# Layer 0's experts: per weight matrix all products of the latent tokens and all of the context tokens, one kind after the other

## The chip, the cores and the metric

One core of a Trainium2 chip runs the whole program. Its engines work side by side, each through its own list of instructions in order: TensorE (PE, matrix products; PEld is its weight loader), VectorE (DVE), ScalarE (ACT), GpSimd (POOL) and SyncE (SP), which issues most of the DMA transfers. The metric is the device time of one execution in microseconds (us), as the median of several.

## The reference

A network of two mixer layers, each followed by a layer of experts, and a second block behind them, all in float32. What matters here is the first layer of experts. It runs over two sets of tokens, 512 latent ones and 256 context ones, with the same 16 experts; each expert takes its best 64 latent tokens (`x`) and its best 32 context tokens (`ctx`).

```python
def expert_choice_ffn(h, router, w_gate, w_up, w_down):
    ...
    cap = CAPACITY_FACTOR * t // N_EXPERTS
    aff = jax.nn.softmax(h.astype(jnp.float32) @ router.astype(jnp.float32), axis=-1)
    gate, idx = lax.top_k(jnp.swapaxes(aff, 1, 2), cap)
    ...
    xs = h[bidx, idx]
    hid = jax.nn.silu(jnp.einsum('becd,edf->becf', xs, w_gate)) * jnp.einsum('becd,edf->becf', xs, w_up)
    y = jnp.einsum('becf,efd->becd', hid, w_down) * gate[..., None].astype(h.dtype)
    return jnp.zeros_like(h).at[bidx, idx].add(y)
```

Each expert has three matrices of 1024x1024: gate, up and down, 4 MB each.

## The kernel before

`moe0` is the stage of layer 0's experts. The tokens of an expert are the stationary operand, the weights stream past them. A matrix comes in four chunks of 1 MB (two row blocks of 128 rows each, `k0` = 0, 2, 4, 6). For each row block there are two latent products, each with 64 tokens against 512 columns of the weights, and four context products, each with 32 tokens against 256 columns. The two latent products write to partitions 0 and 64 on, so they stand side by side in the array; the four context products stand at 0, 32, 64 and 96. In the trace each product leaves two records, so a chunk shows as x8 latent records and x16 context records; in the listings of the program's order one row counts products, x4 and x8.

`expert_gemm` (line 852) runs over the chunks of one matrix: per chunk first the latent products (line 865), then the context ones (line 870), and then `st.done()`, which issues the load of a later chunk into the slot that comes next in a ring of slots. Loads go out on SP's queue (line 832) in the order in which the matrices are used; a load waits until the last product that read its slot is through.

Order of the matrices: gate and up of expert 0; then, for each further expert e+1, gate of e+1 (`product(0, e+1)`), down of e, up of e+1 (`product(1, e+1)`); last, down of expert 15. Results of gate go to `pl0`/`pc0`, of up to `pl1`/`pc1` (names in the trace: `pl`, `pc`), of down to `dl`/`dc` (tiles `ro_lg`). Around them:

- `glu` (line 1068): ACT applies silu to the gate results (into `hl`, `hc`), DVE multiplies by the up results.
- `hidden` (line 1077): TensorE transposes `hl` (four transposes) and `hc` (two), DVE and ACT copy them to `hT`, the stationary operand of the down matrix. It is called ahead of the last chunk of the next expert's gate matrix (`late`, `k == KD - 2`).
- `turn` (line 996): TensorE transposes the gathered tokens `xg` of expert e+2 (eight transposes), DVE and ACT write them to `xT`. It is called ahead of the last chunk of the up matrix.
- behind the down matrix DVE scales the results into `yl` and `yc`, and GpSimd adds them to the tokens in memory by an indirect transfer (lines 1129 to 1135). The stage after this one (retention) loads those tokens.

The order that is written in the code isn't quite the one that runs: a scheduler puts each engine's instructions in order when the program is built, by its own estimate of when their inputs are there, and may interleave what the code writes in sequence.

Of the kernel before, what the change touches and what calls it, by code (L numbers as in the profile page):

```python
# [6 lines left out]
F32 = mybir.dt.float32  # L7
# [4 lines left out]
AF = mybir.ActivationFunctionType  # L12
ALU = mybir.AluOpType
# [4 lines left out]
KD = 8  # L18
# [29 lines left out]
class Net:  # L48
# [658 lines left out]
    CL, CC, E = 64, 32, 16  # L707
# [144 lines left out]
    def expert_gemm(self, st, lat, con, outl, outc, swap=0, late=None, ws=None, done=True):  # L852

        nc = self.nc
        for k0 in range(0, KD, 2):
            w = st.get() if ws is None else ws[k0 // 2]
            if late is not None:
                late(k0)  # L860
            if lat is not None:
                for kk in (k0, k0 + 1):
                    for b in range(2):
                        c = b ^ swap
                        nc.tensor.matmul(outl[64 * b:64 * b + 64, :], lat(kk), w[:, kk - k0, 512 * c:512 * c + 512],  # L865
                                         start=kk == 0, stop=kk == KD - 1)
            if con is not None:
                for kk in (k0, k0 + 1):
                    for b in range(4):
                        nc.tensor.matmul(outc[32 * b:32 * b + 32, :], con(kk), w[:, kk - k0, 256 * b:256 * b + 256],  # L870
                                         start=kk == 0, stop=kk == KD - 1)
            if done:
                st.done()

    def moe0(self, yp, y):


        nc, I = self.nc, self.I
        i, CL, CC, E = 0, self.CL, self.CC, self.E
        CAP = CL + CC  # L880
        rp = self.pool("mo_r", side="right")
        m5l = rp.tile([128, 512], F32, name="mo_m5l")
        m5c = rp.tile([128, 256], F32, name="mo_m5c")
        ii = rp.tile([CAP, E], I32, name="mo_ii")
        si = rp.tile([128, 2, E], I32, name="mo_si")
        gc = rp.tile([128, 2, E], F32, name="mo_gc")
# [8 lines left out]
        g = [self.row(fp, self.modd[i][r, 2 * D:3 * D], f"po_g{r}") for r in range(2)]  # L895
# [32 lines left out]
        st = self.expert_stream(i, order + [(E - 1, "down")])  # L928
# [59 lines left out]
        wk = self.pool("mo_w", 2)  # L988
# [3 lines left out]
        xl2 = self.xl.rearrange("t (b n) -> (t b) n", b=2)  # L992
        xc4 = self.xc.rearrange("t (b n) -> (t b) n", b=4)
        A, B = self.ffnA[i], self.cols[i][:, 3]

        def turn(xg, xT, a=CL, b=CAP):

            for h in range(2):
                tp = tile4()
                for k in range(4):  # L1000
                    kk = 4 * h + k
                    nc.tensor.transpose(tp[:, k, 0:b], xg[:, 128 * kk:128 * kk + 128], self.ident[0:b, 0:b])
                for k in range(4):
# [12 lines left out]

        xT = Xp.tile([128, D], F32, name="X")[:, 0:KD * CL].rearrange("p (k t) -> p k t", k=KD)
        turn(xgs[0], xT, CL, CL)
        no = first(1)
        xg = gather(no, wk.tile([CAP, D], F32, name="xg")[0:CC])  # L1020
# [37 lines left out]
                nc.vector.tensor_copy(si[:, n, 1:E], tr[n][:, 1, 1:E])  # L1058
                nc.vector.tensor_copy(gc[:, n, 1:E], tr[n][:, 2, 1:E])

        def product(n, e, late=None):
            pl = ps.tile([128, 512], F32, name=f"pl{n}")
            pc = ps.tile([128, 512], F32, name=f"pc{n}")[:, 0:256]
            xT = xTs[e]
            self.expert_gemm(st, lambda k: xT[:, k, lat], lambda k: xT[:, k, con], pl, pc, late=late)
            glu(n, e, pl, pc)

        def glu(n, e, pl, pc):
            if n == 0:
                hid[e] = (wk.tile([128, 512], F32, name="hl"), wk.tile([128, 256], F32, name="hc"))  # L1070
                for h, p in zip(hid[e], (pl, pc)):
                    nc.scalar.activation(h, p, AF.Silu)
            else:
                for h, p in zip(hid[e], (pl, pc)):
                    nc.vector.tensor_tensor(h, h, p, ALU.mult)
# [12 lines left out]

        hid, xTs = {}, {}
        tokens = lambda e: gather(ii[:, e:e + 1], wk.tile([CAP, D], F32, name="xg"))  # L1090
        new = lambda: wk.tile([128, KD, CAP], F32, name="xT")
        ps = self.pool("mo_ps", 1, space=PSUM)
        xTc = wk.tile([128, KD, CAP], F32, name="xT")

        def second():
            indices()
            xgs.append(tokens(1))
        for n in range(2):
            ws = [st.get() for _ in range(4)]
# [9 lines left out]
            glu(n, 0, pl, pc)  # L1109
# [5 lines left out]
        xTs[1] = turn(xgs[1], new())  # L1115
        for e in range(E):
            if e + 2 < E:
                xg = tokens(e + 2)
            if e + 1 < E:
                product(0, e + 1, late=lambda k: hidden(e) if k == KD - 2 else None)  # L1120
            else:
                hidden(e)
            dl = psr.tile([128, 512], F32, name="ro_lg", bufs=2)
            dc = psr.tile([128, 512], F32, name="ro_lg", bufs=2)[:, 0:256]
            hTl, hTc = hid[e]
            self.expert_gemm(st, lambda k: hTl[:, k % 4, 64 * (k // 4):64 * (k // 4) + 64],
                             lambda k: hTc[:, k % 2, 32 * (k // 2):32 * (k // 2) + 32], dl, dc)
            yl = wk.tile([128, 512], F32, name="yl")
            nc.vector.scalar_tensor_tensor(yl, dl, gc[:, 0, e:e + 1], m5l, ALU.mult, ALU.mult)  # L1129
            nc.gpsimd.indirect_dma_start(out=xl2, out_offset=bass.IndirectOffsetOnAxis(ap=si[:, 0, e:e + 1], axis=0),  # L1130
                                         in_=yl, in_offset=None, compute_op=ALU.add)
            yc = wk.tile([128, 256], F32, name="yc")
            nc.vector.scalar_tensor_tensor(yc, dc, gc[:, 1, e:e + 1], m5c, ALU.mult, ALU.mult)
            nc.gpsimd.indirect_dma_start(out=xc4, out_offset=bass.IndirectOffsetOnAxis(ap=si[:, 1, e:e + 1], axis=0),
                                         in_=yc, in_offset=None, compute_op=ALU.add)
            if e + 1 < E:
                product(1, e + 1, late=lambda k: xTs.update({e + 2: turn(xg, new())}) if k == KD - 2 and e + 2 < E else None)
        self.warm(ps.tile([128, 512], F32, name="pl0"), yl, 7)
        ps.close()
        psr.close()  # L1140
# [4 lines left out]
        whb.close()  # L1145
        whp.close()
        rp.close()

    def moe1(self, yp, y):

# [1099 lines left out]
```

## Time and profile before

| | |
|---|---|
| median of 3 runs | 2636.24 us (2631.58 to 2636.72) |
| the profiled execution's own time | 2638.1 us |
| its span in the profile | 2636.3 us |
| TensorE busy | 2516.1 us, 95% of the span |
| stage of layer 0's experts 1 to 15 on TensorE | 571.11 to 1128.83 us of the span |

The rows that follow are from the one profiled execution. Times are microseconds from the start of the span. The busy time of TensorE counts a matrix product from its start to its modelled end, so products that overlap are not counted twice, and a small pause between products of two forms can be hidden in a busy engine.

### The profile page before, as it was taken

Reading aid. Unit: us, or ns where it says so; the run is one execution under the profiler, and the core shown is the slowest. Engines: PE = TensorE matmul, PEld = TensorE weight load, DVE = VectorE, ACT = ScalarE, POOL = GpSimd, SP = SyncE. Lnnn points to the kernel's source line nnn. Section 1 sums busy time; section 2 is a strip of 40 time slices with the busy share of each in tenths; the row PEclk is TensorE's granted clock in tenths of the full one; section 3 lists DMA queues with packets and bytes.
Section 4 is the critical chain, followed back from the end, with each engine's and each line's share of the span. In section 5 each row is a group of like instructions: output and inputs, shape, how many; then the busy total and the mean of one; then the engine's idle time right before and its main releaser. Section 6 shows DMA issues by size and latency. Waiting matters only on the chain. (4 is left out here: it accounts for less than half of the span.)

```text
span 2636.3 us, 36600 instructions
## 1 busy us (share of the span) xinstructions
PE 2516.1 (95%) x15122; PEld 1593.6 (60%) x15126; DVE 1089.3 (41%) x2121; ACT 690.5 (26%) x1335; POOL 557.1 (21%) x339
## 2 busy tenths in 40 slices
PE   7999998989999999999999999999998999999999
PEld 6777687833333333368877755444445766788887
DVE  5588686341111111152666332222235458433310
ACT  4322364421010110043224310100004336322211
POOL 2223224311111010023556200000001222122233
PEclk9999998989999999999999899999998999999999
DMA  7226604388999999442463589999982221133331
GB/s 252 80 65 214 234 2 169 137 322 325 395 399 399 390 386 374 156 134 70 146 238 128 218 334 420 419 419 420 419 365 81 98 100 33 56 96 96 120 104 56
DMA packets 145274, 584.80 MB, mean 222 GB/s; under 512 B 17671, under 2 KB 47535, under 8 KB 93908
## 3 DMA queue, kind: packets, MB, share of 16 engines
q1 hardware_dynamic: 138684, 569.87, 56.8%
q0 software_dynamic: 6416, 12.59, 2.2%
q8 instruction: 119, 1.95, 0.3%
q14 instruction: 47, 0.39, 0.0%
q10 hardware_dynamic: 8, 0.01, 0.0%
HBM read 567.70 MB, written 14.71 MB: 221 GB/s over the span
## 5 line engine op out<-in xcount | busy, mean ns | idle before, releaser
L276 POOL TENSOR_TENSOR wlo<-w,whi 128x1024 fp32r<-128x1024 f32 x103 | 271.0, 2632 | 610.6 <-ACT whi L275 610.4
L865 PE MATMUL pl<-w,xT 128*64 128x512 f32 x1240 | 293.0, 601 | 2.7 <-ACT hl L1308 2.7
L275 ACT ACTIVATE whi<-w 128x1024 fp32r<-128x1024 f32 x148 | 154.4, 1050 | 454.6 <-PE acc L296 189.4
L294 PE MATMUL acc<-whi,hhi 128*128 128x512 f32 (+2 forms) x672 | 265.7, 396 | 1.3 <-ACT pre L445 1.1
L295 PE MATMUL acc<-wlo,hhi 128*128 128x512 f32 (+2 forms) x672 | 261.0, 388 | 1.4 <-POOL wlo L276 1.4
L296 PE MATMUL acc<-whi,hlo 128*128 128x512 f32 (+2 forms) x672 | 260.0, 387 | 0.0
L296 PE MATMUL acc<-hhi,wlo 128*128 128x512 f32 (+2 forms) x528 | 198.7, 377 | 3.2 <-POOL wlo L276 3.2
L294 PE MATMUL acc<-hhi,whi 128*128 128x512 f32 (+2 forms) x528 | 198.8, 377 | 2.9 <-DVE hlo L289 1.5
L295 PE MATMUL acc<-hlo,whi 128*128 128x512 f32 (+2 forms) x528 | 199.1, 378 | 0.6 <-POOL hlo L406 0.5
L865 PEld LDWEIGHTS pl<-w,xT 128*64 128x64 f32 x1240 | 86.2, 137 | 149.1 <-issue 133.1
L276 DVE TENSOR_TENSOR wlo<-w,whi 128x1024 fp32r<-128x1024 f32 (+2 forms) x45 | 59.3, 1317 | 255.7 <-ACT whi L275 255.6
L865 PE MATMUL pl<-wb,xT 128*64 128x512 f32 x640 | 152.8, 599 | 0.0
L294 PEld LDWEIGHTS acc<-whi,hhi 128*128 128x128 f32 x672 | 127.5, 190 | 30.1 <-issue 6.1
L295 PEld LDWEIGHTS acc<-wlo,hhi 128*128 128x128 f32 x672 | 127.7, 190 | 27.0 <-POOL wlo L276 3.0
L296 PEld LDWEIGHTS acc<-whi,hlo 128*128 128x128 f32 x672 | 127.4, 190 | 25.5 <-issue 2.4
L164 DVE SCALAR_TENSOR_TENSOR ada_v<-w,csil,ada_v 128x1024 f32<-128x1024 f32 x84 | 132.8, 1616 | 7.6 <-DMA w<-in_ada_w_dram 6.2
L1766 POOL TENSOR_TENSOR X<-X,s_gf 128x1024 f32<-128x1024 f32 x2 | 4.7, 2364 | 515.5 <-DVE X L1292 506.8
L296 PEld LDWEIGHTS acc<-hhi,wlo 128*128 128x128 f32 (+1 forms) x528 | 98.2, 187 | 22.7 <-POOL wlo L276 3.4
L294 PEld LDWEIGHTS acc<-hhi,whi 128*128 128x128 f32 (+1 forms) x528 | 98.3, 186 | 22.4 <-DVE hlo L289 1.7
L295 PEld LDWEIGHTS acc<-hlo,whi 128*128 128x128 f32 (+1 forms) x528 | 98.5, 187 | 19.8 <-POOL hlo L406 0.7
L1012 ACT ACTIVATE xT<-ro_tp,cols,ffnA 128x32 f32<-128x32 f32 x128 | 43.7, 376 | 225.3 <-DVE xT L1009 222.6
L1130 POOL DMA_INDIRECT xl<-yl,mo_si x16 | 25.1, 1568 | 362.7 <-DVE yl L1129 360.9
(599 smaller groups left out, 4272.8 us busy)
## 6 DMA issues: line engine op xcount, KB each, us to landing
w<-in_moe_w_gate_dram SPq DMA_DIRECT2D x91, 1024.0 KB, 13.2
w<-in_moe_w_down_dram SPq DMA_DIRECT2D x84, 1024.0 KB, 14.0
w<-in_moe_w_up_dram SPq DMA_DIRECT2D x68, 1024.0 KB, 12.8
wb<-in_moe_w_up_dram SPq DMA_DIRECT2D x53, 1024.0 KB, 13.3
w<-in_ada_w_dram SPq DMA_DIRECT2D x40, 1024.0 KB, 6.2
wb<-in_moe_w_down_dram SPq DMA_DIRECT2D x38, 1024.0 KB, 11.3
wb<-in_moe_w_gate_dram SPq DMA_DIRECT2D x30, 1024.0 KB, 17.0
w<-in_ret_w_in_dram SPq DMA_DIRECT2D x16, 1024.0 KB, 5.5
```

The lines of the kernel that those rows point to most:

```text
L164: nc.vector.scalar_tensor_tensor(acc[r], w[:, kk], x, acc[r], ALU.mult, ALU.add)
L275: nc.scalar.activation(hi, raw[:, k:k + n, :], AF.Copy)
L276: (nc.vector if fast and (k // n) % 2 == 0 else nc.gpsimd).tensor_sub(lo, raw[:, k:k + n, :], hi.bitcast(F32))
L294: nc.tensor.matmul(out, lh[0], rh[0], start=start, stop=False)
L295: nc.tensor.matmul(out, lh[0], rh[1], start=False, stop=False)
L296: nc.tensor.matmul(out, lh[1], rh[0], start=False, stop=stop)
L865: nc.tensor.matmul(outl[64 * b:64 * b + 64, :], lat(kk), w[:, kk - k0, 512 * c:512 * c + 512], start=kk == 0, stop=kk == KD - 1)
L1012: nc.scalar.activation(xT[:, kk, a:b], tp[:, k, a:b], AF.Identity, scale=A[:, kk, 1:2], bias=B[:, kk, 1:2])
L1130: nc.gpsimd.indirect_dma_start(out=xl2, out_offset=bass.IndirectOffsetOnAxis(ap=si[:, 0, e:e + 1], axis=0), in_=yl, in_offset=None, comput ...
L1766: (nc.gpsimd if t % 3 else nc.vector).tensor_mul(x, x, gf)
```

## The change

In place of `expert_gemm` the three matrices of each expert go through a new function, `expert_runs`: one whole run over the four chunks with products of one kind, then a second run over the same four chunks with the other kind. Which kind comes first alternates from matrix to matrix, so that a matrix begins with the kind with which the one ahead of it ended. All four chunks of a matrix are held through the first run; `st.done()` is called in the second. `hidden` and `turn` are called between the two runs (`between`), and the steps behind the products (`glu`, the scaling and scatter) are called per kind, as soon as its run is through (`after`). Expert 0's own gate and up matrices still go through `expert_gemm`, which there had one kind per call already. (A further function that the change adds, `expert_hidden`, is not called anywhere.)

```diff
+    def latent_gemm(self, lat, w, k0, out, swap=0):
+
+        for kk in (k0, k0 + 1):
+            for b in range(2):
+                c = b ^ swap
+                self.nc.tensor.matmul(out[64 * b:64 * b + 64, :], lat(kk), w[:, kk - k0, 512 * c:512 * c + 512],
+                                      start=kk == 0, stop=kk == KD - 1)
+
+    def context_gemm(self, con, w, k0, out):
...
+    def expert_runs(self, st, lat, con, outl, outc, after, between=None):
...
+        kinds = (0, 1) if self.runs % 2 == 0 else (1, 0)
+        self.runs += 1
+        ws = []
+        for n, kind in enumerate(kinds):
+            if n and between is not None:
+                between()
+            for k0 in range(0, KD, 2):
+                if n == 0:
+                    ws.append(st.get())
+                w = ws[k0 // 2]
+                if kind == 0:
+                    self.latent_gemm(lat, w, k0, outl)
+                else:
+                    self.context_gemm(con, w, k0, outc)
+                if n:
+                    st.done()
+            after[kind]()
...
-        def product(n, e, late=None):
+        def product(n, e, between=None):
             pl = ps.tile([128, 512], F32, name=f"pl{n}")
             pc = ps.tile([128, 512], F32, name=f"pc{n}")[:, 0:256]
             xT = xTs[e]
-            self.expert_gemm(st, lambda k: xT[:, k, lat], lambda k: xT[:, k, con], pl, pc, late=late)
-            glu(n, e, pl, pc)
...
+            self.expert_runs(st, lambda k: xT[:, k, lat], lambda k: xT[:, k, con], pl, pc,
+                             (lambda: glu(n, e, 0, pl), lambda: glu(n, e, 1, pc)), between)
...
+        self.runs = 1
...
             if e + 1 < E:
-                product(0, e + 1, late=lambda k: hidden(e) if k == KD - 2 else None)
+                product(0, e + 1, between=lambda: hidden(e))
             else:
                 hidden(e)
...
-            self.expert_gemm(st, lambda k: hTl[:, k % 4, 64 * (k // 4):64 * (k // 4) + 64],
-                             lambda k: hTc[:, k % 2, 32 * (k // 2):32 * (k // 2) + 32], dl, dc)
...
+            self.expert_runs(st, lambda k: hTl[:, k % 4, 64 * (k // 4):64 * (k // 4) + 64],
+                             lambda k: hTc[:, k % 2, 32 * (k // 2):32 * (k // 2) + 32], dl, dc,
+                             (lambda: last.append(scatter(e, 0, dl)), lambda: scatter(e, 1, dc)))
             if e + 1 < E:
-                product(1, e + 1, late=lambda k: xTs.update({e + 2: turn(xg, new())}) if k == KD - 2 and e + 2 < E else None)
+                product(1, e + 1, between=lambda: xTs.update({e + 2: turn(xg, new())}) if e + 2 < E else None)
```

What the scheduler makes of it on TensorE is seen in the listing of the order. In the rows below L865 (before) and L872 (after) are latent products, L870 and L879 context ones, L1083 and L1111 the transposes of `hidden`, L1002 and L1031 those of `turn`.

First, TensorE early in the stage, before: `pl_5269`/`pc_5270` is the gate matrix of expert 2, `hT_5318`/`hT_5323` the down matrix of expert 1 behind it; `wb`, `ot` and `w` are slots of the ring.

```order
L865 MATMUL pl_5269<-wb,xT 64x512 x4
L870 MATMUL pc_5270<-wb,xT 32x256 x8
L865 MATMUL pl_5269<-wb,xT 64x512 x4
L870 MATMUL pc_5270<-wb,xT 32x256 x8
L865 MATMUL pl_5269<-ot,xT 64x512 x4
L870 MATMUL pc_5270<-ot,xT 32x256 x8
L1083 MATMUL ro_tp<-cs,hl 128x128 x4
L1083 MATMUL ro_tp<-cs,hc 128x128 x2
L865 MATMUL pl_5269<-w_4998,xT 64x512 x4
L870 MATMUL pc_5270<-w_4998,xT 32x256 x8
L865 MATMUL ro_lg<-w_5001,hT_5318 64x512 x4
L870 MATMUL ro_lg<-w_5001,hT_5323 32x256 x8
```

The same matrices after the change, `hT_5300`/`hT_5295` being the down matrix:

```order
L872 MATMUL pl_5269<-wb,xT 64x512 x8
L872 MATMUL pl_5269<-ot,xT 64x512 x4
L872 MATMUL pl_5269<-w_4998,xT 64x512 x4
L1111 MATMUL ro_tp<-cs,hl 128x128 x4
L1111 MATMUL ro_tp<-cs,hc 128x128 x2
L879 MATMUL pc_5270<-wb,xT 32x256 x16
L879 MATMUL pc_5270<-ot,xT 32x256 x8
L879 MATMUL pc_5270<-w_4998,xT 32x256 x8
L879 MATMUL ro_lg<-w_5001,hT_5300 32x256 x8
L879 MATMUL ro_lg<-wb,hT_5300 32x256 x24
L872 MATMUL ro_lg<-w_5001,hT_5295 64x512 x4
L872 MATMUL ro_lg<-wb,hT_5295 64x512 x12
```

Here the two kinds have been moved apart, and the gate matrix ends with the kind with which the down matrix begins.

Second, TensorE late in the stage, at the gate matrix of expert 12 (`pl_7539`/`pc_7540`), after the change. Before it, the products stand there chunk by chunk, four latent and eight context ones, as in the first listing.

```order
L872 MATMUL pl_7539<-w,xT 64x512 x4
L1111 MATMUL ro_tp<-cs,hl 128x128 x4
L1111 MATMUL ro_tp<-cs,hc 128x128 x2
L879 MATMUL pc_7540<-w,xT 32x256 x5
L872 MATMUL pl_7539<-w,xT 64x512 x4
L879 MATMUL pc_7540<-w,xT 32x256 x11
L1031 MATMUL ro_tp<-cs,xg 128x96
L872 MATMUL pl_7539<-w,xT 64x512 x4
L879 MATMUL pc_7540<-w,xT 32x256 x8
L1031 MATMUL ro_tp<-cs,xg 128x96 x4
L872 MATMUL pl_7539<-w,xT 64x512 x4
L879 MATMUL pc_7540<-w,xT 32x256 x8
```

Here the scheduler has put the two runs into each other again, chunk by chunk, and has cut one context chunk into five products and three.

Third, TensorE at the end of the stage, before: `pc_8333` is the last up matrix, `hT_8389`/`hT_8394` the last down matrix, and line 113 the products behind it that wait for `yl`.

```order
L870 MATMUL pc_8333<-ot,xT 32x256 x8
L1083 MATMUL ro_tp<-cs,hl 128x128 x4
L1083 MATMUL ro_tp<-cs,hc 128x128 x2
L865 MATMUL ro_lg<-ot,hT_8389 64x512 x4
L870 MATMUL ro_lg<-ot,hT_8394 32x256 x8
L865 MATMUL ro_lg<-w_8095,hT_8389 64x512 x4
L870 MATMUL ro_lg<-w_8095,hT_8394 32x256 x8
L865 MATMUL ro_lg<-w_8109,hT_8389 64x512 x4
L870 MATMUL ro_lg<-w_8109,hT_8394 32x256 x8
L865 MATMUL ro_lg<-w_8123,hT_8389 64x512 x4
L870 MATMUL ro_lg<-w_8123,hT_8394 32x256 x8
L113 MATMUL pl_8452<-yl,cs 128x512 x7
```

The same place after the change, `pl_8332` being the latent products of the last up matrix; behind these rows come eight more context products and line 113.

```order
L872 MATMUL pl_8332<-ot,xT 64x512 x4
L1111 MATMUL ro_tp<-cs,hl 128x128 x4
L1111 MATMUL ro_tp<-cs,hc 128x128 x2
L872 MATMUL ro_lg<-ot,hT_8389 64x512 x4
L872 MATMUL ro_lg<-w_8114,hT_8389 64x512 x4
L879 MATMUL ro_lg<-ot,hT_8394 32x256 x7
L872 MATMUL ro_lg<-w_8120,hT_8389 64x512 x4
L879 MATMUL ro_lg<-ot,hT_8394 32x256
L879 MATMUL ro_lg<-w_8114,hT_8394 32x256 x8
L879 MATMUL ro_lg<-w_8120,hT_8394 32x256
L872 MATMUL ro_lg<-w_8126,hT_8389 64x512 x4
L879 MATMUL ro_lg<-w_8120,hT_8394 32x256 x7
```

The last up matrix now ends with its latent products, straight ahead of the transposes that need them, and behind the last latent products of the stage there are now fifteen context products in place of eight.

SP's list of loads is the same before and after, and behind this stage all five engines have the same instructions in the same order.

## Rows read from the trace of the kernel before

**Rows 1.** The page: span, and TensorE's busy time.

```profile
span 2636.3 us, 36600 instructions
PE 2516.1 (95%) x15122; PEld 1593.6 (60%) x15126; DVE 1089.3 (41%) x2121; ACT 690.5 (26%) x1335; POOL 557.1 (21%) x339
```

**Rows 2.** One stretch of the stage: busy per engine, granted clock, DMA share, GB/s.

```profile
core 0: us, PE busy (x) PEld busy (x) DVE busy (x) ACT busy (x) POOL busy (x), PEclk, DMA share, GB/s
645.00:682.00 37.00, 37.00 (x319) 12.58 (x318) 6.26 (x16) 4.65 (x14) 4.08 (x3) 1.00 1.03 394
```

**Rows 3.** Timeline of TensorE over one expert: start, duration, line, operation.

```profile
622.52 1.94 PE L865 MATMUL ro_lg<-w,hT 128*64 128x512 f32 x8
624.39 1.07 PE L870 MATMUL ro_lg<-w,hT 128*32 128x256 f32 x16
625.39 1.94 PE L865 MATMUL ro_lg<-wb,hT 128*64 128x512 f32 x8
...
654.88 0.66 PE L1083 MATMUL ro_tp<-cs,hl 128*128 128x128 f32 x4
...
655.69 1.94 PE L865 MATMUL pl<-w,xT 128*64 128x512 f32 x8
...
658.55 1.94 PE L865 MATMUL ro_lg<-w,hT 128*64 128x512 f32 x8
```

**Rows 4.** Timeline of TensorE at expert 0, one kind per run.

```profile
542.64 6.22 PE L865 MATMUL pl<-w,X 128*64 128x512 f32 x26
548.80 0.68 PE L1002 MATMUL ro_tp<-cs,xg 32*128 32x32 f32 x8
...
552.13 3.66 PE L870 MATMUL pc<-w,xT 128*32 128x256 f32 x64
555.72 3.22 PE L865 MATMUL pl<-wb,X 128*64 128x512 f32 x13
...
560.63 1.07 PE L865 MATMUL pl<-ot,X 128*64 128x512 f32 x2
561.64 0.62 PE L870 MATMUL pc<-wb,xT 128*32 128x256 f32 x2
562.19 0.30 PE L1057 MATMUL ro_tp<-cs,yl 16*128 16x16 f32 x4
```

**Rows 5.** Timeline of TensorE at the end of the stage.

```profile
1114.91 1.07 PE L870 MATMUL pc<-ot,xT 128*32 128x256 f32 x16
1115.91 0.66 PE L1083 MATMUL ro_tp<-cs,hl 128*128 128x128 f32 x4
...
1117.35 1.94 PE L865 MATMUL ro_lg<-ot,hT 128*64 128x512 f32 x8 [0.33 <-DVE hT L1085]
...
1127.83 1.07 PE L870 MATMUL ro_lg<-w,hT 128*32 128x256 f32 x16
1128.83 6.28 PE L113 MATMUL pl<-yl,cs 128*128 128x512 f32 x14
1140.11 3.33 PE L113 MATMUL acc<-rs_r,cs 128*128 128x128 f32 x14 [5.01 <-DVE rs_r L101]
```

**Rows 6.** Timeline of DVE at the end of the stage.

```profile
1115.09 0.69 DVE L1075 TENSOR_TENSOR hl<-hl,pl 128x512 f32<-128x512 f32 x1 [10.02 <-PE pl L865]
...
1127.94 0.75 DVE L1129 SCALAR_TENSOR_TENSOR yl<-ro_lg,mo_gc,mo_m5l 128x512 f32<-128x512 f32 x1 [10.65 <-PE ro_lg L865]
```

**Rows 7.** DMA queues from 690 to 836 us: packets, MB, share of 16 engines.

```profile
q1 hardware_dynamic: 7486, 54.53, 92.3%
q0 software_dynamic: 1600, 3.15, 9.5%
```

**Rows 8.** One load of a gate matrix on SP's queue, and its use on TensorE.

```profile
636.75 1.56 SPq L832 DMA_DIRECT2D wb<-in_moe_w_gate_dram  x3
...
682.31 1.94 PE L865 MATMUL pl<-wb,xT 128*64 128x512 f32 x8
```

**Rows 9.** DMA issues from 690 to 836 us: count, size, median us to landing.

```profile
w<-in_moe_w_gate_dram SPq DMA_DIRECT2D x11, 1024.0 KB, 23.3
```

More of the change, by code (lines that the diff above doesn't have):

```diff
@@ L852, in expert_gemm @@
     def expert_gemm(self, st, lat, con, outl, outc, swap=0, late=None, ws=None, done=True):
-        nc = self.nc
         for k0 in range(0, KD, 2):
@@ L861, in expert_gemm @@
             if lat is not None:
[L862 to L866, printed above, removed]
+                self.latent_gemm(lat, w, k0, outl, swap)
             if con is not None:
[L868 to L871, printed above, removed]
+                self.context_gemm(con, w, k0, outc)
             if done:
                 st.done()
+    def latent_gemm(self, lat, w, k0, out, swap=0):
[5 more added lines that the diff above has]
+    def context_gemm(self, con, w, k0, out):
+        for kk in (k0, k0 + 1):
+            for b in range(4):
+                self.nc.tensor.matmul(out[32 * b:32 * b + 32, :], con(kk), w[:, kk - k0, 256 * b:256 * b + 256],
+                                      start=kk == 0, stop=kk == KD - 1)
+    def expert_runs(self, st, lat, con, outl, outc, after, between=None):
[12 more added lines that the diff above has]
+                else:
+                    self.context_gemm(con, w, k0, outc)
+                if n:
+                    st.done()
+            after[kind]()
     def moe0(self, yp, y):
@@ L1064, in product, with glu @@
             xT = xTs[e]
-            self.expert_gemm(st, lambda k: xT[:, k, lat], lambda k: xT[:, k, con], pl, pc, late=late)
-            glu(n, e, pl, pc)
-        def glu(n, e, pl, pc):
+            self.expert_runs(st, lambda k: xT[:, k, lat], lambda k: xT[:, k, con], pl, pc,
+                             (lambda: glu(n, e, 0, pl), lambda: glu(n, e, 1, pc)), between)
+        def glu(n, e, kind, p):
             if n == 0:
-                hid[e] = (wk.tile([128, 512], F32, name="hl"), wk.tile([128, 256], F32, name="hc"))
-                for h, p in zip(hid[e], (pl, pc)):
-                    nc.scalar.activation(h, p, AF.Silu)
-            else:
-                for h, p in zip(hid[e], (pl, pc)):
-                    nc.vector.tensor_tensor(h, h, p, ALU.mult)
+                if e not in hid:
+                    hid[e] = (wk.tile([128, 512], F32, name="hl"), wk.tile([128, 256], F32, name="hc"))
+                nc.scalar.activation(hid[e][kind], p, AF.Silu)
+            else:
+                nc.vector.tensor_tensor(hid[e][kind], hid[e][kind], p, ALU.mult)
         def hidden(e):
@@ L1108, in moe0 @@
             self.expert_gemm(st, None, lambda k: xTc[:, k, 0:CC], None, pc, ws=ws)
-            glu(n, 0, pl, pc)
+            glu(n, 0, 0, pl)
+            glu(n, 0, 1, pc)
         pp.close()
@@ L1115, in moe0, with scatter @@
         xTs[1] = turn(xgs[1], new())
+        self.runs = 1
+        def scatter(e, kind, p):
+            y, g, m5, dst = (("yl", gc[:, 0, e:e + 1], m5l, xl2), ("yc", gc[:, 1, e:e + 1], m5c, xc4))[kind]
+            y = wk.tile([128, p.shape[-1]], F32, name=y)
+            nc.vector.scalar_tensor_tensor(y, p, g, m5, ALU.mult, ALU.mult)
+            nc.gpsimd.indirect_dma_start(out=dst, out_offset=bass.IndirectOffsetOnAxis(ap=si[:, kind, e:e + 1], axis=0),
+                                         in_=y, in_offset=None, compute_op=ALU.add)
+            return y
+        last = []
         for e in range(E):
@@ L1125, in moe0 @@
             hTl, hTc = hid[e]
-            self.expert_gemm(st, lambda k: hTl[:, k % 4, 64 * (k // 4):64 * (k // 4) + 64],
-                             lambda k: hTc[:, k % 2, 32 * (k // 2):32 * (k // 2) + 32], dl, dc)
[L1128 to L1135, printed above, removed]
+            self.expert_runs(st, lambda k: hTl[:, k % 4, 64 * (k // 4):64 * (k // 4) + 64],
+                             lambda k: hTc[:, k % 2, 32 * (k // 2):32 * (k // 2) + 32], dl, dc,
+                             (lambda: last.append(scatter(e, 0, dl)), lambda: scatter(e, 1, dc)))
             if e + 1 < E:
-                product(1, e + 1, late=lambda k: xTs.update({e + 2: turn(xg, new())}) if k == KD - 2 and e + 2 < E else None)
+                product(1, e + 1, between=lambda: xTs.update({e + 2: turn(xg, new())}) if e + 2 < E else None)
+        yl = last[-1]
         self.warm(ps.tile([128, 512], F32, name="pl0"), yl, 7)
@@ L1147, in moe0, with expert_hidden @@
         rp.close()
+    def expert_hidden(self, wk, ps, pl):
+        nc = self.nc
+        hl = wk.tile([128, 512], F32, name="hl", bufs=1)
+        nc.scalar.activation(hl, pl[0], AF.Silu)
+        nc.vector.tensor_tensor(hl, hl, pl[1], ALU.mult)
+        hTl = wk.tile([128, 4, 128], F32, name="hTl", bufs=1)
+        tp = ps.tile([128, 4, 128], F32, name="tp", bufs=3)
+        for b in range(4):
+            nc.tensor.transpose(tp[:, b, :], hl[:, 128 * b:128 * b + 128], self.ident)
+        nc.vector.tensor_copy(hTl, tp)
+        return hTl
     def moe1(self, yp, y):
```

## The prediction

> **What bounds the kernel now.** The page comes first: TensorE is busy for 2516.1 of 2636.3 us [rows 1], so what TensorE does not have to do may shorten the time, where it waits for nothing else. The change touches one stage, the experts 1 to 15 of layer 0, so the view by stretches is next. In a stretch of 37 us TensorE is busy for 37.00 at granted clock 1.00, 2.4 GHz, but the DMA share reads 1.03 as well, at 394 GB/s [rows 2]. Two resources look full, and the question is which of them would have to be late for TensorE to stop. The timeline of TensorE shows why a busy engine can still have something to save: a chunk's latent products take 1.87 us from their start to that of the context products (622.52 to 624.39), these 1.00 (to 625.39), and so on without a gap, so that one expert lasts 36.03 us (622.52 to 658.55) [rows 3]. Busy does not tell whether the time goes into products or into changing from one kind to the other.
>
> **The price of a change of kind.** Expert 0 ran one kind at a time already. There 26 latent records, 13 products, take 6.16 us (542.64 to 548.80); at two side by side that is seven slots. A chunk has two slots and takes 1.87. With s a slot and o what a run costs besides, 7s + o = 6.16 and 2s + o = 1.87: s = 0.858, o = 0.154. The 64 context records are eight slots of four products in 3.59 us (552.13 to 555.72), against two slots in 1.00: s = 0.432, o = 0.137 [rows 3, 4]. The 64 records cross three chunk borders, and these leave no trace in the sum, so o belongs to the change of kind: 0.146 us on the mean of the two.
>
> A product without its neighbours takes a whole slot: one alone lasts 1.01 us (560.63 to 561.64), which is 0.858 + 0.154, and one context product 0.55 (561.64 to 562.19), near 0.432 + 0.137 [rows 4].
>
> **The sum.** I counted the listing of the new order on TensorE from the first product of expert 1 to the last of expert 15. If the code's order ran, 46 matrices with one change each inside would leave about 46 changes in place of 367, some 47 us less. The listing has 189: six for expert 1, three each for experts 2 to 6, five and eleven for 7 and 8, and then 21 for each expert (26 in the last, with its second down matrix), where 24 stood (32). The grouping holds for the first half of the stage only; after it the runs are put into each other again.
>
> - Changes of kind: 178 fewer at 0.146: -25.9 us.
> - Runs cut at odd places: eight latent runs of an odd number lose half a slot each (3.4), and cut context chunks lose five slots (2.2): +5.6.
> - Seven places where transposes stand between two runs of the same kind, so that the array changes over twice for no change of kind: 7 x 0.146 = +1.0.
> - The transposes themselves are the same in number. A set of six takes 0.81 us (654.88 to 655.69) [rows 3]. They come in 45 blocks where there were 43, at most a change each: +0.3.
> - The last `hidden`: before, DVE's product for `hl` started 0.18 us behind the last latent products and took 0.69, under the 1.00 us of the context products (1114.91 to 1115.91) [rows 5, 6]. These stand ahead of the latent ones now, the cover is gone, and TensorE waits: +1.0. The earlier calls of `hidden` have a whole run, at least 1.7 us, or a context chunk as before, between the product and the transposes, and the DVE step with its start is 0.9; I cost them at nothing.
> - The end: the next stage starts from `yl`. DVE took it up 0.11 us behind the last latent products (1127.83, 1127.94), and TensorE took up its new work at 1140.11, a chain from `yl` on [rows 5, 6]. What counts is thus the end of the last latent run. Behind it stood 1.00 us of context products (1127.83 to 1128.83) and now stand four slots, 4 x 0.432 + 0.137 = 1.87: this much less of TensorE's work is ahead of `yl`, -0.9.
>
> Together -18.9 us. The profiled execution took 2638.1, 1.8 more than its span and 1.9 more than the median; 2638.1 - 18.9 = 2619.2 by its own time, and **2617.3 us** by the median. An early expert should then last 33.0 us: twelve chunks at 1.72 + 0.86, twice 0.81 of transposes, three changes.
>
> **The loads.** All of a matrix's chunks are held longer, and they are used sooner. SP's queue moved 54.53 MB in 146 us [rows 7]: 52 chunks of 1.05 MB, 2.81 us each, 33.7 per expert with the gathers and scatters (3.15 MB, 9.5% of the engines) beside them. Before, TensorE took 36.03 and so the loads ran ahead more and more; at 33.0 they lose 0.7 per expert, some 4 us over the six grouped experts. A load's lead was smallest early in the stage: issued at 636.75 and used at 682.31, 45.6 us [rows 8], of which the longest median to landing is 23.3 [rows 9], so 22 are left. A context-first run wants the fourth chunk 2.6 us behind the first in place of 8.6: 6 us less. A latent-first run frees the first chunk after 6.9 + 1.0 in place of 2.9: 5 us later. 22 - 4 - 6 - 5 leaves 7 us. The queue keeps the same order and, being behind by some 20 us, doesn't run dry when a slot is freed 5 us later. I cost the loads at nothing, with the least cover of all the terms.
>
> The unknown prices: transposes behind latent products and ahead of context ones do not occur before (17 times now); if the array changes over there at no more cost, or at one more change, it is 2.5 us either way. The cut runs may cost nothing, when the other kind's products take the free columns (-5.6), though [rows 4] speak against. In-order queues of DVE and ACT can make TensorE wait at `hidden` and at the first use of `xT`: from 0 to the 1.0 us of the last `hidden` at each of two places in seven experts, +14. I take the first end, since those steps come in the same order as their inputs.
>
> **The rivals.**
> - Small waits eat half: 10 us of the +14 above, 2627. For it: each engine's queue was put in order by an estimate that takes the loads to be late, as the re-mixed second half shows. Against: DVE was busy for 6.26 of 37 us and ACT for 4.65 [rows 2].
> - The loads become the bound. Without the 4 us that 33.7 against 33.0 costs, the lead is 22 - 6 - 5 = 11 us, 1.8 for each of six experts; TensorE begins to wait when the loads take over 34.8 us per expert, 2.90 per chunk. At 36.0 the fourteen experts from the low point on take 14 x 36.0 - 11 = 493 us, against 14 x 36.03 = 504 before and 485 by my sum: 8 more, 2625. From 37.2 on, 3.1 us per chunk, it is slower than before: 14 x 37.2 - 11 = 510, 2642. Measured is 33.7 [rows 7]. The Trainium skill, "DMA: Bandwidth & Descriptors", section "Where 436 GB/s comes from", has the HBM side bind loads at about 358 GB/s; by that rate an expert's 12.58 MB and 0.79 MB of gathers and scatters are an estimated 37.3 us, and the time would be about 2643. The trace does not agree: 394 GB/s in this stage [rows 2].
> - The price belongs to a block of products on a chunk, not to the change of kind. The number of blocks stays, no gain comes, and the other terms stand: 5.6 + 1.0 + 0.3 + 1.0 - 0.9 = +7.0, 2643. It decides if a context chunk behind a context chunk still takes 1.00 us. Against it are the 64 records in 3.59 [rows 4].
> - The stage is shorter but the next one starts on something else, and the time stays 2636. Against: its start follows `yl` through the scatter.
> - The code's order runs after all, 47 us less: 2590. The listing is the program's, so hardly.
>
> **How the numbers follow.** Forecast 0.76, small waits 0.11, loads 0.05 (0.01 of it slower), price by chunk 0.03, no gain 0.04, full grouping 0.01. A change of under 0.2%, 5.3 us, is what a measurement of this kernel can't tell from none. Faster: 0.76 + 0.11 + 0.04 + 0.01 = 0.92; same 0.04; slower 0.04. The range takes the free cut runs and cheap transposes at the low end, 2617.3 - 5.6 - 1.7 = 2610, and the small waits at the high end, 2627.
>
> **What would show it.** Early experts at 33.0 us each and late ones at 35.6 (three changes fewer) or a little more; context chunks inside a run at 0.86 and latent ones at 1.72; the stage's last product near 1111; a wait of about 1 us ahead of the last `hidden`; no waits of TensorE for loads. Wrong would be: a wait for a DMA of several us in experts 4 to 8, 0.5 to 1 us of waiting for DVE or ACT at each `hidden`, or late experts longer than 36.03, from the cut runs.

## The result, and the profile after

| | before | after |
|---|---|---|
| median of 4 runs each | 2636.48 us | 2617.05 us (2611.34 to 2618.19) |
| ratio | | 0.9926, 95% interval 0.9906 to 0.9945 |
| the profiled execution's own time, its span | 2638.1, 2636.3 us | 2618.19, 2616.4 us |
| first product of expert 1 to the end of the last one of expert 15 | 572.55 to 1128.83: 556.28 us | 572.43 to 1110.76: 538.33 us |

The change made the kernel faster by 0.74%, 19.4 us by the medians. The prediction had said 2617.3, in a range of 2610 to 2627. The stage itself became 17.95 us shorter. "The stage" below always means the last row of the table, from its first product on; the start of 571.11 that was given for the kernel before counts eight transposes ahead of that product.

The page of the changed kernel (answers to [rows 1]):

```profile
span 2616.4 us, 36613 instructions
PE 2496.6 (95%) x15126; PEld 1612.8 (62%) x15126; DVE 1089.2 (42%) x2121; ACT 690.6 (26%) x1335; POOL 556.5 (21%) x339
```

The view by stretches, over the same 37 us as in [rows 2]:

```profile
645.00:682.00 37.00, 37.00 (x278) 14.87 (x275) 5.53 (x13) 4.27 (x12) 4.07 (x3) 1.00 1.02 389
```

TensorE lost 19.5 us of busy time and is still busy for every microsecond of the stretch. A busy share thus cannot show this gain; the timeline of TensorE can (start, duration, operation; answers to [rows 3]):

```profile
615.55 0.66 PE L1111 MATMUL ro_tp<-cs,hl 128*128 128x128 f32 x4
...
616.35 1.93 PE L879 MATMUL pc<-wb,xT 128*32 128x256 f32 x32
618.10 1.05 PE L879 MATMUL pc<-ot,xT 128*32 128x256 f32 x16
618.97 1.05 PE L879 MATMUL pc<-w,xT 128*32 128x256 f32 x16
619.83 1.05 PE L879 MATMUL ro_lg<-w,hT 128*32 128x256 f32 x16
...
667.68 7.09 PE L872 MATMUL pl<-w,xT 128*64 128x512 f32 x32
674.60 5.32 PE L872 MATMUL pl<-wb,xT 128*64 128x512 f32 x24
...
747.58 0.66 PE L1111 MATMUL ro_tp<-cs,hl 128*128 128x128 f32 x4
...
954.37 0.66 PE L1111 MATMUL ro_tp<-cs,hl 128*128 128x128 f32 x4
...
1027.01 0.66 PE L1111 MATMUL ro_tp<-cs,hl 128*128 128x128 f32 x4
```

The start of a row to the start of the next one is what the operation really took. A context chunk behind a context chunk takes 0.87 us (618.10 to 618.97), where it took 1.00 behind latent products. Eight latent slots, 32 records, take 6.92 (667.68 to 674.60), and at 674.60 one matrix ends and the next begins with nothing between them. The `hidden` rows are milestones: four early experts take 615.55 to 747.58, 33.01 us each, in place of 36.03. Two late ones take 954.37 to 1027.01, 36.32 each, as long as late ones took before (below).

The end of the stage, TensorE and then DVE (answer to [rows 5, 6]; in brackets the idle time before the row and what ended it):

```profile
1094.95 1.94 PE L872 MATMUL pl<-ot,xT 128*64 128x512 f32 x8
1097.73 0.65 PE L1111 MATMUL ro_tp<-cs,hl 128*128 128x128 f32 x4 [0.85 <-DVE hl L1103]
...
1099.17 1.94 PE L872 MATMUL ro_lg<-ot,hT 128*64 128x512 f32 x8 [0.57 <-DVE hT L1113]
...
1108.90 1.93 PE L879 MATMUL ro_lg<-w,hT 128*32 128x256 f32 x30
1110.76 6.28 PE L113 MATMUL pl<-yl,cs 128*128 128x512 f32 x14
1120.63 3.33 PE L113 MATMUL acc<-rs_r,cs 128*128 128x128 f32 x14 [3.59 <-DVE rs_r L101]
```

```profile
1109.02 0.75 DVE L1150 SCALAR_TENSOR_TENSOR yl<-ro_lg,mo_gc,mo_m5l 128x512 f32<-128x512 f32 x1 [9.91 <-PE ro_lg L872]
```

`yl` is taken up at 1109.02 in place of 1127.94, 18.92 us earlier, and TensorE starts its next work 19.48 us earlier (1120.63, before 1140.11). All of the gain goes on into the span.

The waits of TensorE between 565 and 1115 us (us in total, times, longest):

```profile
PE ro_tp L1031 <- DMA xg<-hd,mo_ii: 5.1, 1, 5.1
PE ro_tp L1111 <- DVE hl L1103: 0.8, 1, 0.8
PE ro_lg L872 <- DVE hT L1113: 0.6, 1, 0.6
```

The first is ahead of the stage, the other two are the last `hidden`. No load and no earlier `hidden` stops TensorE.

### The profile page after: what moved, and what is told of

The parts are those of the page before. It is cut to its first block, busy times and chain, and to the rows that moved or that the text cites. A ratio compares the mean times of both kernels' runs of the same rounds, so it can differ in the third digit from the quotient of the medians.

```text
span 2616.4 us, 36613 instructions
## 1 busy us (share of the span) xinstructions
PE 2496.6 (95%) x15126; PEld 1612.8 (62%) x15126; DVE 1089.2 (42%) x2121; ACT 690.6 (26%) x1335; POOL 556.5 (21%) x339
## 5 line engine op out<-in xcount | busy, mean ns | idle before, releaser
L872 PE MATMUL pl<-w,xT 128*64 128x512 f32 x1240 | 289.0, 599 | 2.7 <-ACT hl L1355 2.7
L872 PEld LDWEIGHTS pl<-w,xT 128*64 128x64 f32 x1240 | 90.4, 137 | 159.1 <-issue 148.8
L872 PE MATMUL pl<-wb,xT 128*64 128x512 f32 x640 | 151.4, 597 | 0.0
L872 PEld LDWEIGHTS pl<-wb,xT 128*64 128x64 f32 x640 | 47.7, 137 | 81.4 <-issue 75.3
```

The lines of the kernel that those rows point to most:

```text
L872: self.nc.tensor.matmul(out[64 * b:64 * b + 64, :], lat(kk), w[:, kk - k0, 512 * c:512 * c + 512], start=kk == 0, stop=kk == KD - 1)
```

## Experiments

The theory is that of the prediction: each change between latent and context products costs TensorE about 0.146 us, and loads are ahead of their use. The rivals are a price that belongs to something else that changes at the same place (chunk, result tile, tokens), and loads that become the bound when TensorE goes faster. The runs are compared by the stage first: its start alone moves between 567.57 and 576.01 us from run to run, with TensorE's wait for `xg` ahead of it.

### The code's order, on all 15 experts

The scheduler had kept the grouping in the first half only. Here each run and the transposes between two runs are queued behind the last product ahead of them on TensorE (an edge that fixes the order of issue and adds no wait):

```diff
             if n and between is not None:
-                between()
-            for k0 in range(0, KD, 2):
...
+                with self.behind():
+                    between()
+            with self.behind():
+                for k0 in range(0, KD, 2):
...
+            self.ran = p.ins
...
+    def behind(self):
+        return contextlib.nullcontext() if self.ran is None else self.tc.issue_after(self.ran)
```

> The changed kernel with the order that the code writes made fast on TensorE for all 15 experts: each run of products stands behind the one ahead of it, and the transposes between the two runs stand between them. The listing has 46 changes of kind in place of 189, no cut runs, and no transposes between two runs of one kind. Price by the change of kind (0.146 us), loads hidden: -20.9 (143 changes), -5.6 (cut runs), -1.0 (same-kind breaks) = -27.5 against the changed kernel, about 2589.6 us, every expert at 33.0 us. Loads become the bound (33.7 us per expert): the experts of the second half last 33.7 us or more, TensorE shows waits for DMA of 6 us or more together, and the time is 2596 or above. Price by the block of products on a chunk: only the cut runs go, about 2610.

Measured: 2590.46 us, ratio to the kernel before 0.9826 (0.9810 to 0.9842); the stage 508.79 us (575.99 to 1084.78). The timeline of its TensorE, in the second half and at the end:

```profile
911.04 0.66 PE L1122 MATMUL ro_tp<-cs,hl 128*128 128x128 f32 x4
...
977.05 0.66 PE L1122 MATMUL ro_tp<-cs,hl 128*128 128x128 f32 x4
...
1072.73 0.66 PE L1122 MATMUL ro_tp<-cs,hl 128*128 128x128 f32 x4 [0.85 <-DVE hl L1114]
...
1084.78 6.28 PE L114 MATMUL pl<-yl,cs 128*128 128x512 f32 x14
```

Between the first two rows lie two experts in 66.01 us, 33.0 each, as early ones take; no load stops TensorE. That is the price by the change of kind. This kernel is faster than both others; the intervals do not overlap.

### No alternation

```diff
-        kinds = (0, 1) if self.runs % 2 == 0 else (1, 0)
+        kinds = (0, 1)
```

> The same fixed order, but every matrix begins with its latent run, so each border between two matrices is a change of kind too: 91 changes in place of 46. Price by the change of kind: 45 x 0.146 = +6.6 us on the kernel with the fixed order, and the last up matrix now ends with context products, which gives back most of the 1.0 us wait ahead of the last hidden, so about +5.8, 2595.4 if the other lands at 2589.6. If a change of kind beside a change of matrix costs nothing (the matrix border has its own start that hides it): no difference, or 1 us less.

Measured: 2593.27 us (0.9824 to 0.9857); the stage 571.75 to 1085.93, 514.18 us, 5.39 longer than with the alternation. The medians, 2.8 us apart, have intervals that overlap, so the stage is the better witness. The 0.85 us ahead of the last `hidden` is gone, and 0.34 of the 0.56 behind it is left; without these waits the difference is 6.5 us for 45 changes, 0.144 each. A border between two matrices does not hide a change.

### Twice as many changes

```diff
                 for kk in (k0, k0 + 1):
-                    for b in range(2):
...
+                    with self.behind(con):
+                        for b in range(2):
...
+                    self.ran = p.ins
+                    if con is not None:
+                        self.context_block(con, w, k0, kk, outc)
```

> The kernel before with the two kinds alternating per row block in place of per chunk: two latent products, four context products, and so on, in a fixed order. Same products, same slots, same order of the loads; 735 changes of kind in place of 367. Price by the change of kind: +368 x 0.146 = +53.7 us, about 2690. Price by the chunk (a block of products that begins on a new slot of weights): within a chunk nothing is added, 2636.

Measured: 2695.11 us, ratio 1.0230 (1.0212 to 1.0248). The stage goes from 571.60 to 1184.20 (the last product starts at 1183.56 and takes 0.64): 612.60 us, 56.3 more than before, 0.153 per change. Part of this is waiting: TensorE waits for DVE at the `hidden` calls, 2.7 us in all, where the kernel before waited 0.33 (from 565 to 1185 us: us in total, times, longest):

```profile
PE ro_tp L1098 <- DVE hl L1090: 2.2, 7, 0.3
PE ro_lg L867 <- DVE hT L1100: 0.6, 1, 0.6
```

Without the waits it is 53.9 us, 0.147 per change. In the timeline a row block is two slots in 1.58 us (644.98 to 646.56), 0.858 + 0.432 + 0.29:

```profile
644.98 1.08 PE L867 MATMUL pl<-w,xT 128*64 128x512 f32 x4
645.99 0.64 PE L882 MATMUL pc<-w,xT 128*32 128x256 f32 x8
646.56 1.08 PE L867 MATMUL pl<-w,xT 128*64 128x512 f32 x4
```

The price is paid inside a chunk as well, so it does not belong to the chunk.

### The same alternation, one shape

```diff
-                    for b in range(4):
-                        nc.tensor.matmul(outc[32 * b:32 * b + 32, :], con(kk), w[:, kk - k0, 256 * b:256 * b + 256],
...
+                    for b in range(2):
+                        nc.tensor.matmul(outc[64 * b:64 * b + 64, :], con(kk), w[:, kk - k0, 512 * b:512 * b + 512],
...
-            self.expert_gemm(st, lambda k: xT[:, k, lat], lambda k: xT[:, k, con], pl, pc, late=late)
+            self.expert_gemm(st, lambda k: xT[:, k, lat], lambda k: xT[:, k, lat], pl, pc, late=late)
```

> The kernel before in its own order, kinds alternating per chunk, but the context products have the shape of the latent ones (the latent tokens again, 64 tokens by 512 columns, two per row block, into the context results; the context part of the output is therefore not computed). Each chunk is four slots of 0.858 = 3.43 us. If the price of 0.146 belongs to the change of the products' shape, there is none now outside the transposes: 184 chunks x 3.432 = 631.5 in place of 184 x 2.580 + 367 x 0.146 = 528.3, +103 us, about 2740. If it belongs to the change of the result tile and the stationary tokens, which still alternate, the 53.6 us stay: +157, about 2793.

Measured: 2740.42 us, ratio 1.0396 (1.0378 to 1.0413); the stage 573.95 to 1236.45, 662.50 us, 106.2 more than before, where 103 and 157 were the two answers. Every product has the latent tokens here, also where the context's stood, so the context results are not computed. The rows still alternate between `pl` and `pc` on the same chunk:

```profile
646.79 1.89 PE L865 MATMUL pl<-ot,xT 128*64 128x512 f32 x8
648.51 1.89 PE L875 MATMUL pc<-ot,xT 128*64 128x512 f32 x8
650.22 1.89 PE L865 MATMUL pl<-w,xT 128*64 128x512 f32 x8
651.94 1.89 PE L875 MATMUL pc<-w,xT 128*64 128x512 f32 x8
```

Each takes 1.71 or 1.72 us, two slots and nothing else. Result tile and chunk change freely; the price belongs to the change of shape, from products of 64 tokens against 512 columns to products of 32 against 256 and back. Tokens and columns change together in every run, so which of the two the price hangs on stays open.

### Fewer slots for the loads

To learn how much lead the loads had left, slots were taken from the ring of 20, on the code's order (three, five, ten) and on the changed kernel (five):

```diff
-        wb1 = self.pool("mo_wb1", self.NB0[1], side="right")
-        st.open(lambda: whp.tile([128, WSLOT], F32, name="w2"), whp.bufs - 3, ii[0:1, 1:2])
-        st.open(lambda: wb1.tile([128, WSLOT], F32, name="wb"), wb1.bufs, ii[0:1, 1:2])
```

(Three fewer leaves the second of these lines in; ten fewer takes out the two lines that open `ot` and `whb` as well.)

> The kernel with the fixed code order, with three slots fewer in the ring of loads (the three of wb1). A load is then issued up to three slots later, 3 x 2.81 = 8.4 us. If the lead of the loads is as small as the prediction says (7 us left in the grouped experts; in the fixed order it falls further, by 33.7 - 33.2 = 0.5 us for each of the ten experts behind, to about 2), TensorE has to wait for loads, about 6 us in all, 2590.5 + 6 = 2597. If the lead was much larger than that (over 10 us at the end): no waits, 2590.5.

> The same with five slots fewer, 5 x 2.81 = 14.1 us of lead: with 2 us left in the fixed order, 12 us of waits for loads in TensorE, 2602.5; with 10 us left, 4 us, 2594.5; with over 14, 2590.5. Together with the run of three fewer the two times bracket the lead that was left: each slot taken away beyond it should cost 2.8 us, and none before it.

> The changed kernel as it is, with the same five slots fewer (14.1 us of lead). With the 7 us of lead that the prediction left: 7 us of waits for loads, about 2624. With 11 us left: 3 us, 2620. With over 14: 2617, the same. In the kernel before, with 22 us left, it would cost nothing.

> The fixed code order with ten slots of 20. With 20 slots SP's queue waits for earlier loads to land, with 15 it waits for TensorE to free slots, and neither makes TensorE wait. With ten slots a slot comes round every 10 x 2.76 = 27.6 us, of which about 6.6 lie between its first product and its release, so 21 us are left for issue, queue and landing. If only the DMA's rate sets when a load lands: still no waits, stage 508.8 to 512. If a slot less is 2.8 us less of lead once the queue no longer waits for landings (from some seven slots fewer on): three slots too few, 8.4 us less of lead against some 5 to 7 left, 2 to 10 us of waits.

| kernel | median us, interval of the ratio | stage us |
|---|---|---|
| code's order, 20 slots | 2590.46, 0.9810 to 0.9842 | 508.79 |
| 17 slots | 2585.70, 0.9795 to 0.9839 | 508.79 (568.73 to 1077.52) |
| 15 slots | 2590.51, 0.9816 to 0.9862 | 508.69 (572.64 to 1081.33) |
| 10 slots | 2596.11, 0.9823 to 0.9859 | 520.54 (572.74 to 1093.28) |
| changed kernel, 15 slots | 2613.65, 0.9909 to 0.9951 | 537.54 (568.75 to 1106.29) |

The first three expectations, from the lead that the prediction had left, were 2597, up to 2602.5 and 2624. None of these came; the other branch of each did, a lead larger than that: five slots fewer cost nothing. SP's waits from 690 to 836 us say why. First the changed kernel with its 20 slots (its four largest of eleven), then the code's order with 15 (its four largest of six):

```profile
SPq L832 <- DMA w<-in_moe_w_down_dram: 25.3, 9, 3.9
SPq L832 <- DMA w<-in_moe_w_gate_dram: 25.1, 11, 2.9
SPq L832 <- DMA w<-in_moe_w_up_dram: 16.8, 8, 2.1
SPq L832 <- DMA wb<-in_moe_w_down_dram: 16.7, 6, 3.7
```

```profile
SPq L833 <- PE pc L881: 46.9, 17, 8.3
SPq L833 <- PE pl L873: 32.5, 12, 6.2
SPq L833 <- PE ro_lg L873: 24.8, 10, 4.9
SPq L833 <- PE ro_lg L881: 20.7, 7, 10.9
```

With 20 slots SP's queue waits 123.6 us for earlier loads to land and only 1.3 for TensorE to free a slot. Slots were free when it came to them, and a slot freed later delays nothing. What makes the queue wait for earlier loads while slots are free, no run shows. (The kernel before, with the same 20 slots and the slower TensorE, waited for both: 51.5 us for TensorE, most of it in the row below, and 75.4 for loads.)

```profile
SPq L832 <- PE pc L870: 36.5, 22, 3.3
```

With 15 slots the queue waits for TensorE, the median from issue to landing falls (loads of gate matrices into `w`: 21.8 us with 20 slots, 14.8 with 15), and the loads land as before, since the DMA's rate sets that. So a queue that waits for slots does not yet make TensorE wait. At ten slots it does: the stage is 11.75 us longer, a little more than the 2 to 10 expected.

### More loads

The rate itself was tested with 13 loads more that nobody reads, each behind the first load of a gate matrix (the half chunks have `0:1` for `0:2`):

```diff
-            nc.sync.dma_start(t, I["moe_w_" + w][i, e, k // 2])
+            p = nc.sync.dma_start(t, I["moe_w_" + w][i, e, k // 2])
+            if i == 0 and self.spare is not None and (w, k) == ("gate", 0):
+                with self.tc.issue_after(p.ins):
+                    nc.sync.dma_start(self.spare[:, 0:2], I["moe_w_gate"][0, 0, 0][:, 0:2])
```

> The kernel with the fixed code order, one slot of the ring used for 13 loads more of half a chunk (0.5 MB), each behind the first load of a gate matrix, which nobody reads (17 slots remain, which alone changed nothing: the stage from the first product of expert 1 to the last of expert 15 was 508.8 us with 20 and with 17 slots). If the loads go at the DMA's own rate (2.81 us per MB, 33.7 us per expert) and are ahead of TensorE by little (7 us at the end: the 22 of the prediction, less 4 and 6, less 0.5 for each of ten experts): 13 x 1.4 = 18.3 us more of loads, 18.3 - 7 = 11 us of waits, stage 520, time about 2598 to 2601. If the DMA has rate to spare: stage 508.8, no change.

> The same with 13 whole chunks (1 MB) more: 36.5 us of loads more. At the DMA's own rate the second half megabyte is paid in full, 18.3 us more than the run with half: stage 538, 2616 to 2620. If the DMA has rate to spare: stage 508.8.

> The kernel before with the same 13 whole chunks more. Its experts took 36.03 us and the loads would take 33.7 + 2.8 = 36.5 per expert: 13 x 0.5 = 6 us more than TensorE, with 22 us of lead to take them from. So no change, stage 556.3, 2634 to 2636, if the lead was 22 us. If the loads were already the bound there, 2650 or above.

Measured on the code's order: with half chunks 2606.01 us (0.9859 to 0.9898), the stage 570.41 to 1096.26, 17.1 us longer; with whole chunks 2619.43 (0.9917 to 0.9957), the stage 567.57 to 1107.59, 31.2 longer. On the kernel before: 2633.81, ratio 0.9988 (0.9976 to 1.0001), the stage 569.06 to 1127.35, 2.0 longer; its waits of TensorE name ACT's copies into `hT` with 2.0 us and no load. From 690 to 836 us the DMA moved as much without the loads more (first row, the kernel before) as with them (second, whole chunks on the code's order):

```profile
DMA packets 9099, 57.86 MB, mean 396 GB/s; under 512 B 1022, under 2 KB 1534, under 8 KB 2430
DMA packets 9163, 57.74 MB, mean 395 GB/s; under 512 B 1036, under 2 KB 1623, under 8 KB 2519
```

So the loads do go at the DMA's own rate. Before the change a whole megabyte per expert fitted beside TensorE; in the code's order it costs 31.2 of the 36.5 us that it takes, which would leave about 5.3 us of lead. The half chunks cost 17.1 of their 18.3, more than the 11 us expected, and by the same difference would leave only 1.2, so the lead is known to no better than that. The idle time in the seven rows that wait for a load adds up to 10.98. Some 6 us more are lost, an estimated 5 of them behind the two longest of these waits, where the granted clock was at or near 0.50 for about 10 us (the last section shows it on the run with whole chunks).

### The last up matrix

```diff
-        kinds = (0, 1) if self.runs % 2 == 0 else (1, 0)
+        kinds = (0, 1) if self.runs % 2 == 0 or self.runs == 3 * self.E - 3 else (1, 0)
```

> The kernel with the fixed code order, but the last up matrix begins with its latent run, so that its context products cover DVE's last product for hl, as they did before the change. Two changes of kind more (+0.3), and the waits of TensorE ahead of the last hidden and the last down matrix (0.85 + 0.56 us in the fixed order) fall to the 0.33 of the kernel before (-1.1): -0.8, about 2589.7, too little for the time alone; the rows should show it. If the wait comes from something else than DVE's product behind the latent run, it stays at 0.85.

Measured: 2587.26 us (0.9802 to 0.9840), which the time alone cannot tell from 2590.46; the stage 576.01 to 1084.13, 508.12 us, 0.67 shorter.

```profile
1071.11 1.04 PE L881 MATMUL pc<-ot,xT 128*32 128x256 f32 x16
1072.08 0.66 PE L1122 MATMUL ro_tp<-cs,hl 128*128 128x128 f32 x4
...
1073.52 1.94 PE L873 MATMUL ro_lg<-ot,hT 128*64 128x512 f32 x8 [0.39 <-DVE hT L1125]
```

The wait of 0.85 is gone: it was DVE's product for `hl` without cover.

## Why the prediction was right, point by point

**The price of a change.** Right, and now held by five orders of the same products:

| kernel | changes of kind | the same, transposes counted as a third kind | waits of TensorE inside, us | stage us |
|---|---|---|---|---|
| code's order | 46 | 77 | 1.4 | 508.79 |
| no alternation | 91 | 121 | 0.3 | 514.18 |
| changed | 189 | 241 | 1.4 | 538.33 |
| before | 367 | 410 | 0.3 | 556.28 |
| per row block | 735 | 784 | 2.7 | 612.60 |

From 46 to 367 it is 47.5 us for 321 changes, 0.148 each; from 367 to 735, without the waits, 0.147. If a change to or from a block of transposes is counted as well and the waits are taken out, the four orders without cut runs lie near one line: 0.147 each from 77 to 121, 0.146 to 410, 0.144 to 784. The one-shape run shows that it belongs to the shape. The Trainium skill, "TensorEngine Tiling (Array Packing)", section "Key Properties", says that changing the tiling mode, and not just the tile, drains TensorE; the runs agree, and put about 0.146 us to it here.

**178 changes fewer.** Right, and what they gained, net of the cut runs, lies all in the first half. 33.01 us for an early expert is 3.02 less, and 21 x 0.146 is 3.07. In the second half the step had the wrong level, though not the wrong difference. The prediction expected late experts at 35.6 "or a little more" and called anything over 36.03 a sign against it; they take 36.32. The 36.03 was an early expert's. Late experts of the kernel before, whose transposes stand in more blocks, took longer (timeline of its TensorE):

```profile
971.51 0.66 PE L1083 MATMUL ro_tp<-cs,hl 128*128 128x128 f32 x4
...
1044.20 0.66 PE L1083 MATMUL ro_tp<-cs,hl 128*128 128x128 f32 x4
```

72.69 us for two, 36.35 each. Three changes fewer gain 0.44 in each late expert, and a cut context chunk (0.22), a same-kind break (0.15) and the transposes' further blocks (0.07) take as much back. The sum had these terms, so it came out right; the sign of being wrong had left them out.

**Cut runs and breaks (+5.6, +1.0).** Right, as far as one can tell. The changed kernel lies above the line of the other four: without waits its stage is 29.5 us longer than that of the code's order, and 164 changes (third column) at 0.146 are 23.9. The 5.6 left are what the prediction had for the cut runs; breaks and extra blocks are among the 164. The code's order has 30 blocks of transposes in place of 45, which its expectation left out: some 2.2 us, and so the stage fell by 29.54 in place of 27.5. That a change to transposes costs as much as the others is taken from the fit, and the terms were not tried singly.

**The last `hidden` (+1.0) and the end (-0.9).** Right: TensorE waits 0.85 + 0.57 us there in place of 0.33, 1.1 more; `yl` moved by 18.92, 0.97 more than the stage's length; 0.12 of that is the stage's earlier start.

**The loads at nothing.** Right in the result, wrong in one step of the working. The step said that a latent-first run frees the first chunk 5 us later and took these 5 us from the lead. In the changed kernel SP's queue waits for landings and hardly for slots, so a slot freed later took nothing, and with that step left out its own sum gives 22 - 4 - 6 = 12 us. In the code's order ten later experts lose about 0.7 us each from the same low point on, which would leave 5; the loads added above leave 1.2 or 5.3. No run measured the lead itself. The term with the least cover was thus better covered than stated, but by rate the rival was near. 33.7 us of loads stand against 33.0 of TensorE in a grouped expert, and half a megabyte more per expert already made TensorE wait. The loads moved at 389 GB/s in the stretch shown above. The bound of about 358 that the prediction quoted from the Trainium skill ("DMA: Bandwidth & Descriptors", section "Where 436 GB/s comes from") is not what this one core shows.

**Small waits.** None: the three rows of waits above are all that there is.

**The number.** The sum without its last term has the stage 18.0 us shorter, and it is 17.95. That the median came out within 0.3 us of the forecast is partly luck, since single runs lie between 2611.34 and 2618.19.

## What to carry to other kernels

Where products of two shapes alternate, price the change from two run lengths in the trace that is there, and count the changes in the order that really runs: here the scheduler gave back more than half of what the code's order was worth, and an edge that fixes the order was worth 27 us more. Whether loads can keep up is a question of two rates, us per expert of each side. How many slots the ring has, and when one is freed, cannot matter while the load queue does not wait for slots; here it cost nothing with 15 slots, where the queue did wait, and 11.75 us with ten. A test by "so many us per expert" needs the level of the same part of the kernel before, not of another part.

## What was not expected of the hardware

A wait for a load can cost more than its length. In the run with 13 whole chunks more TensorE waited 3.18 and then 1.33 us for a gate matrix; the stretches ahead of, in and behind these waits (columns as in [rows 2]):

```profile
980.00:989.00 9.00, 9.00 (x108) 4.42 (x108) 3.46 (x10) 2.60 (x8) 0.95 (x1) 1.00 1.03 392
993.00:997.00 4.00, 2.39 (x31) 1.01 (x32) 0.00 (x0) 0.00 (x0) 0.00 (x0) 0.65 1.01 416
997.00:1001.00 4.00, 4.00 (x20) 1.87 (x14) 0.69 (x1) 0.76 (x2) 0.00 (x0) 0.50 1.00 418
1001.00:1005.00 4.00, 4.00 (x22) 1.30 (x20) 0.00 (x0) 0.00 (x0) 0.00 (x0) 1.00 1.02 422
```

```profile
993.29 1.09 PE L885 MATMUL pc<-w,xT 128*32 128x256 f32 x16 [3.18 <-DMA w<-in_moe_w_gate_dram]
995.70 1.93 PE L885 MATMUL pc<-w,xT 128*32 128x256 f32 x16 [1.33 <-DMA w<-in_moe_w_gate_dram]
997.57 1.12 PE L1126 MATMUL ro_tp<-cs,hl 128*128 128x128 f32 x4
```

The granted clock falls from 1.00 to 0.50, from 2.4 to 1.2 GHz, for at least 4 us behind the waits, and comes back with TensorE busy. At half clock a context chunk takes 1.87 us (995.70 to 997.57) in place of 0.87, and the four transposes 1.12 in place of 0.66. So the late loads cost this run time in two ways. With half chunks the clock was at 0.50 behind the waits of 3.06 and 3.30 us and stayed at 1.00 behind the five shorter ones, of 0.35 to 1.71. The same shows at the stage's own start in the changed kernel, where TensorE waits 5.1 us for `xg` and the clock is at 0.50 from 570 to 576 us.
